# Mixer B's softmax division on GpSimd instead of VectorE

## The chip, the cores and the metric

The kernel runs on one core of one Trainium2 chip. The metric is the device time of one execution in microseconds (us), given as the median of several runs. Engines are named as in the profile: PE is TensorE (its matmuls; PEld its weight loads), DVE is VectorE, ACT is ScalarE, POOL is GpSimd, SP is SyncE, whose queue issues most of the DMAs.

## The reference

A two-layer encoder on 512 tokens of width 1024. Layer 0 mixes tokens by dilated window attention (mixer A), layer 1 by multi-head latent attention (mixer B). Each mixer is followed by a dense squared-ReLU MLP. The change is in mixer B alone, and of it only in the last three lines:

```python
def mla_mixer(h, w_in, q_a_gain, w_qb, kv_a_gain, w_kvb, q_gain, k_gain, w_o):
    lat = h @ w_in                                   # c_q (256), c_kv (128), k_rope (64)
    ...
    q = (rms_norm(c_q, q_a_gain) @ w_qb).reshape(B, S, 8, 192)
    kv = (rms_norm(c_kv, kv_a_gain) @ w_kvb).reshape(B, S, 8, 256)
    ...                                              # per-head RMS norm of q and k, rotary part of 64
    def attend(qblk):
        s = jnp.einsum('bqhd,bkhd->bhqk', qblk, k).astype(jnp.float32) * scale
        p = jax.nn.softmax(s, axis=-1)
        return jnp.einsum('bhqk,bkhd->bqhd', p.astype(v.dtype), v)
```

The output of the 8 heads goes through `w_o`, is added to the input, and the second MLP follows.

## The kernel before

Everything is float32. Products that need full precision are split into a high and a low part (`whi`, `wlo` and the like), three matmuls each. Tiles of 128 rows; the 512 tokens are four row blocks `r`.

**Mixer B.** The 8 heads are worked as four pairs `p` of two heads `h`. For each pair there are, per row block, a projection of keys and values (`kv_chunk`, three matmuls of 512 columns) and one of queries (`q_chunk`, six matmuls of 384 columns), both at line 1032 into the two PSUM banks `sc`. ACT takes the squares for the norm (L1043 for queries, L137 for keys), DVE adds a constant (L129, `rs_v`), POOL raises to the power -1/2 (L132: `rqs` for queries, `krs` for keys). DVE and POOL then make the rotary parts (queries: L1050, L1053 on DVE, `rd` at L1057 on POOL; keys: `ks` at L1086 on DVE, `kd` at L1088 on POOL). PE transposes them (L124 into the two banks `tp`), and ACT and DVE write them as high and low parts (`qn`, `qr`, `kn`, `kr`, L1069 to L1103).

**One step of attention** is one head and one row block, 32 steps in all. `score` does five matmuls (L1114) into a bank `acc`; DVE reduces the maximum (L1116) and scales it (L1117); ACT takes the exponential into the SBUF tile `pe` and its sum (L1119); DVE inverts the sum (L1120) and multiplies `pe` by it (L1121). Three steps later `part2` has PE transpose `pe` (four matmuls of 128x128 at L124 into a bank `acc`), and DVE (even `r`) or ACT (odd `r`) copies the result to `pTs` (L1132, L1130). After the fourth row block of a head, `pv_b` multiplies by the values (L1138) and ACT and DVE write the two parts of `oB` (L1140, L1141; named `hT` in the profile). `pe` has three buffers. The four banks `acc` are shared by scores, transposes and values; in the last pair the scores use `sc` and the rest `tp`, because `acc` then holds the output projection `w_o` (L185), which runs between the steps as far as its weights are split (L157 ACT, L158 DVE).

**Order.** The code gives an order of calls (the table `plan` puts the next pair's projections between the steps of this one), but each engine's final order is chosen by a scheduler when the program is built; it may move an instruction ahead of others on its engine, and it decides anew when an operation changes its engine. On the chip each engine then works strictly in that order and waits where an input or a buffer is not ready. In the names below a number marks one use of a buffer: `pe_8842` is one step's tile, `acc_8985` one use of a bank.

Of the kernel before, what the change touches and what calls it, by code (L numbers as in the profile page):

```python
# [13 lines left out]
ALU = mybir.AluOpType  # L14
# [73 lines left out]
def encoder_kernel(ctx: ExitStack, tc: tile.TileContext, x, norm_mix, norm_ffn, a_w_qkv, a_q_gain, a_k_gain,  # L88
# [3 lines left out]
    V, A, G, PE = nc.vector, nc.scalar, nc.gpsimd, nc.tensor  # L92
# [3 lines left out]
    def nm(s):  # L96
        uid[0] += 1
        return f"{s}_{uid[0]}"
# [24 lines left out]
    def transpose(o, i):  # L123
        PE.transpose(o, i, ident)  # L124
# [826 lines left out]
    if True:  # L951
        with tc.tile_pool(name="bpool", bufs=1, reuse_waits="tile") as bp, \
# [66 lines left out]
            def bank(d, which):  # L1019

                pool, tag = {"s": (sc_p, "sc"), "p": (tp_p, "tp"), "o": (tp_p, "tp")}[which] \
                    if d["p"] == HB // 2 - 1 else (acc_p, "acc")
                return pool.tile([P, 512], F32, tag=tag, name=nm(tag))
# [82 lines left out]
            def score(d, h, r):  # L1106

                qn, qr, kn, kr = d["qn"][r], d["qr"][r], d["kn"], d["kr"]
                rq = d["rq"][:, r, h:h + 1]
                sc = bank(d, "s")  # L1110
                ops = [(qn[:, h, 0], kn[:, h, 0]), (qn[:, h, 0], kn[:, h, 1]), (qn[:, h, 1], kn[:, h, 0]),
                       (qr[:, h], kr[:, h, 0]), (qr[:, h], kr[:, h, 1])]
                for i, (lt, rt) in enumerate(ops):
                    PE.matmul(sc, lhsT=lt, rhs=rt, start=(i == 0), stop=(i == 4))  # L1114
                mx = st.tile([P, 4], F32, tag="bmx", name=nm("bmx"))
                V.tensor_reduce(mx[:, 0:1], sc, axis=AX.X, op=ALU.max)  # L1116
                V.tensor_scalar(mx[:, 1:2], mx[:, 0:1], rq, -1.0, op0=ALU.mult, op1=ALU.mult)  # L1117
                pe = bw.tile([P, S], F32, tag="pe", name=nm("pe"), bufs=3)
                A.activation(pe, sc, AF.Exp, bias=mx[:, 1:2], scale=rq, accum_out=mx[:, 2:3])  # L1119
                V.reciprocal(mx[:, 3:4], mx[:, 2:3])  # L1120
                V.tensor_scalar(pe, pe, mx[:, 3:4], None, op0=ALU.mult)  # L1121

                def part2(pT):
                    tp = bank(d, "p")
                    for j in range(NT):
                        transpose(tp[:, j * P:(j + 1) * P], pe[:, j * P:(j + 1) * P])
                    tv = tp.rearrange("p (j t) -> p j t", j=NT)
                    dst = pT[:, :, r * P:(r + 1) * P]
                    if r % 2:
                        A.activation(dst, tv, AF.Copy)  # L1130
                    else:
                        V.tensor_copy(dst, tv)  # L1132
                return part2
# [27 lines left out]
            for s_ in range(HB * NT + lag):  # L1161
                p, c = divmod(s_, 8)
                if s_ < HB * NT:
                    if c == 0 and p:
                        cur = nxt
                    pend.append((cur, c // 4, c % 4, score(cur, c // 4, c % 4)))
                if s_ >= lag:
                    d, h2, r2, f = pend.pop(0)
                    if r2 == 0:
                        if pTs is None:  # L1170
                            pTs = x16.tile([P, 2, NT, S], F32, tag="x16", name="pTs")
                        pT = pTs[:, h2]
                    f(pT)
                    if r2 == NT - 1:
                        pv_b(d, h2, pT)
                if p + 1 < HB // 2:
                    if c == 2:
                        nxt = new_pair(p + 1)
                    if s_ < NT - 1:
                        tail = tail + [q_chunk(cur, s_ + 1)]  # L1180
                    fresh = [fn(nxt, r) for fn, r in plan.get(c, [])]
                    if c == 7:
                        tail, fresh = tail + fresh, []
                    for f in tail:
                        f()
                    tail = fresh
# [40 lines left out]
```

## Time and profile before

| | us |
|---|---|
| median of 3 runs (lowest, highest) | 1428.91 (1428.28, 1428.96) |
| span of the profiled execution | 1425.8 |
| what lies between the two | 3.1 |
| PE busy | 1394.0 (98%) |
| DVE, ACT, POOL busy | 939.6, 740.5, 217.2 |
| mixer B's attention, about | 925 to 1060 of the span |

No time is listed for the profiled execution but its span; the 3.1 us beside it are the median less that span. The granted TensorE clock was full in every slice. A matmul's end is modelled and overlaps the next one's start, so idle time of PE shorter than about 0.15 us does not show. The useful measure of PE is the spacing in the chain of work, where five score matmuls take 1.16 us although each is listed with 390 ns.

### The profile page before, as it was taken

The page shows a single profiled execution, that of the slowest core. Times are in us where ns is not written, and L with a number is a line of the kernel's source. Part 1 is how long each engine was busy: PE and PEld are TensorE (multiplying, and loading weights), DVE is VectorE, ACT ScalarE, POOL GpSimd, SP SyncE. Part 2 cuts the span into 40 slices and gives each one's busy share as a digit, 9 for nine tenths or more (in the row PEclk, how much of TensorE's full clock was granted, in tenths as well). Part 3 has the DMA queues.
Part 4 walks back from the last instruction along what each step waited for, and adds up shares of the span by engine and source line. Part 5 has one row for each costly group of instructions (what it writes and reads, how often), then busy time and mean ns, then how long its engine had stood idle before and what let it go on. Part 6 is the DMA issues. An engine that isn't in the chain of part 4 may idle for free.

```text
span 1425.8 us, 19234 instructions
## 1 busy us (share of the span) xinstructions
PE 1394.0 (98%) x7044; PEld 1183.8 (83%) x7044; DVE 939.6 (66%) x1497; ACT 740.5 (52%) x1594; POOL 217.2 (15%) x240
## 2 busy tenths in 40 slices
PE   7999999999999999999999999999999999999998
PEld 7999888988888988888888887777768888888886
DVE  6886768676886754465564759788745365575647
ACT  6554656464564623553545446677633553544543
POOL 1110212021112001020010203433201020020201
PEclk9999999999999999999999999999999999999999
DMA  9535222322322335668493844200115658394835
GB/s 323 166 134 168 75 87 87 107 89 75 118 61 77 121 134 195 174 133 222 116 233 99 206 120 91 82 31 30 44 40 163 183 127 231 93 234 128 192 90 118
DMA packets 121086, 185.25 MB, mean 130 GB/s; under 512 B 8416, under 2 KB 58336, under 8 KB 120992
## 3 DMA queue, kind: packets, MB, share of 16 engines
q1 hardware_dynamic: 101808, 144.96, 31.6%
q0 software_dynamic: 19184, 39.07, 15.2%
q8 instruction: 55, 0.90, 0.3%
q14 instruction: 39, 0.32, 0.1%
HBM read 176.13 MB, written 7.86 MB: 129 GB/s over the span
## 4 chain that ended last, share of the span: by engine, by line
PE 89%; DVE 6%; ACT 2%; issue 1%; DMA 1%; POOL 0%; SPq 0%; DVEq 0%; ACTq 0%; POOLq 0%
PE acc L185 51%; PE sc L852 11%; PE tp L852 7%; PE tp L124 4%; PE sc L421 3%; PE acc L1138 1%; PE sc L1032 1%; PE acc L1114 1%; PE tp L421 1%; DVE wlo L796 1%; PE sco L701 1%; PE sc L587 1%; PE acc L421 1%; PE sco L697 1%; DVE wlo L407 1%
## 5 line engine op out<-in xcount | busy, mean ns | idle before, releaser
L185 PE MATMUL acc<-whi,hT 128*128 128x512 f32 (+2 forms) x1216 | 384.2, 390 | 2.2 <-ACT hT L739 1.3
L185 PE MATMUL acc<-hT_f,whi 128*128 128x512 f32 (+1 forms) x1152 | 318.7, 366 | 1.7 <-DVE resid L915 1.2
L158 DVE TENSOR_TENSOR wlo<-raw,whi 128x1024 fp32r<-128x1024 f32 (+3 forms) x146 | 172.4, 1189 | 180.2 <-ACT whi L157 179.9
L185 PEld LDWEIGHTS acc<-whi,hT 128*128 128x128 f32 x1216 | 225.4, 188 | 42.0 <-ACT hT L739 1.9
L185 PEld LDWEIGHTS acc<-hT_f,whi 128*128 128x128 f32 x1152 | 208.1, 189 | 37.4 <-DVE resid L915 1.6
L185 PE MATMUL acc<-wlo,hT 128*128 128x512 f32 (+2 forms) x608 | 235.9, 388 | 0.0
L157 ACT ACTIVATE whi<-raw 128x1024 fp32r<-128x1024 f32 (+3 forms) x146 | 149.7, 1031 | 161.5 <-PE acc L185 64.1
L796 DVE TENSOR_TENSOR wlo<-wqs,whi 128x1024 fp32r<-128x1024 f32 x112 | 137.9, 1232 | 113.4 <-ACT whi L795 113.4
L185 PE MATMUL acc<-hT_f,wlo 128*128 128x512 f32 (+1 forms) x576 | 204.9, 366 | 0.0
L795 ACT ACTIVATE whi<-wqs 128x1024 fp32r<-128x1024 f32 x112 | 118.8, 1061 | 161.3 <-PE acc L185 65.8
L852 PE MATMUL sc<-whi,asp 128*128 128x512 f32 x512 | 164.9, 390 | 0.8 <-DVE resid L826 0.7
L781 POOL DMA_DIRECT2D wqs<-in_ffn_w_dram x64 | 77.6, 1344 | 546.1 <-DVE wlo L796 362.4
L185 PEld LDWEIGHTS acc<-wlo,hT 128*128 128x128 f32 x608 | 114.4, 188 | 18.7 <-issue 0.2
L185 PEld LDWEIGHTS acc<-hT_f,wlo 128*128 128x128 f32 x576 | 108.5, 189 | 17.4
L852 PE MATMUL tp<-whi,asp 128*128 128x512 f32 x352 | 112.2, 390 | 1.8 <-DVE resid L826 1.8
L852 PEld LDWEIGHTS sc<-whi,asp 128*128 128x128 f32 x512 | 96.1, 188 | 21.4 <-issue 1.5
L132 POOL TENSOR_TENSOR qrs<-rs_v,nhalf 128x4 f32<-128x4 f32 x48 | 58.7, 1228 | 288.8 <-DVE rs_v L129 239.7
L852 PE MATMUL sc<-wlo,asp 128*128 128x512 f32 x256 | 99.6, 389 | 0.0
L137 ACT ACTIVATE junk<-acc 128x128 f32<-128x128 f32 x192 | 53.0, 276 | 56.4 <-PE acc L185 51.4
L852 PEld LDWEIGHTS tp<-whi,asp 128*128 128x128 f32 x352 | 66.1, 188 | 16.4 <-DVE resid L826 2.7
L852 PE MATMUL tp<-wlo,asp 128*128 128x512 f32 x176 | 68.2, 389 | 0.0
L295 ACT ACTIVATE qkT<-tp 128x512 f32<-128x512 f32 x48 | 35.8, 765 | 51.2 <-PE tp L124 50.9
(231 smaller groups left out, 2185.3 us busy)
## 6 DMA issues: line engine op xcount, KB each, us to landing
wqs<-in_ffn_w_dram SPq DMA_DIRECT2D x80, 512.0 KB, 5.1
raw<-in_ffn_w_dram SPq DMA_DIRECT2D x64, 512.0 KB, 4.5
wqs<-in_ffn_w_dram POOLq DMA_DIRECT2D x64, 512.0 KB, 7.5
raw<-in_a_w_qkv_dram SPq DMA_DIRECT2D x96, 256.0 KB, 3.1
b<-in_a_w_qkv_dram SPq DMA_DIRECT2D x24, 384.0 KB, 5.7
vall<-vo POOLq DMA_DIRECT2D x24, 192.0 KB, 2.2
raw<-in_a_w_o_dram SPq DMA_DIRECT2D x8, 512.0 KB, 3.8
raw<-in_b_w_o_dram SPq DMA_DIRECT2D x8, 512.0 KB, 3.7
```

The costliest lines, as they stand in the source:

```text
L124: PE.transpose(o, i, ident)
L132: G.tensor_tensor(out, v[:, :n], nhalf[:, :n], op=ALU.pow)
L137: A.activation(junk, x, AF.Square, scale=1.0 / math.sqrt(dim), accum_out=out)
L157: A.activation(hi[:, :nk, :n], raw[:, :nk, :n], AF.Copy)
L158: V.tensor_tensor(lo[:, :nk, :n], raw[:, :nk, :n], hi[:, :nk, :n].bitcast(F32), op=ALU.subtract)
L185: PE.matmul(accs[o][:, oc], lhsT=lt, rhs=rt, start=(kt == 0 and p_i == 0 and hv == 0), stop=(kt == total - 1 and p_i == 2), skip_group_che ...
L295: A.activation(dst, tv, AF.Copy)
L421: PE.matmul(banks[t][:, :VH], lhsT=lt, rhs=rt[:, j], start=(first and k == 0 and i_ == 0), stop=(k == 3 and i_ == 2), skip_group_check=True)
L781: marks["sum"] = nc.gpsimd.dma_start(t, src, accum_op=ALU.add).ins
L795: A.activation(hi, x, AF.Copy)
L796: V.tensor_tensor(lo, x, hi.bitcast(F32), op=ALU.subtract)
L852: PE.matmul(bk[t], lhsT=lt, rhs=rt[:, j], start=(first and k == 0 and i_ == 0), stop=(k == 3 and i_ == 2), skip_group_check=True)
```

## The change

The multiplication by the inverse sum, on DVE before, is issued on POOL. It reads and writes the SBUF tile `pe`; the operations of DVE that read PSUM stay where they are.

```diff
                 A.activation(pe, sc, AF.Exp, bias=mx[:, 1:2], scale=rq, accum_out=mx[:, 2:3])
                 V.reciprocal(mx[:, 3:4], mx[:, 2:3])
-                V.tensor_scalar(pe, pe, mx[:, 3:4], None, op0=ALU.mult)
+                G.tensor_scalar(pe, pe, mx[:, 3:4], None, op0=ALU.mult)
```

POOL gets 32 instructions and DVE loses 32; ACT keeps its 984 rows and SP's queue is the same, row by row. The scheduler's order differs through mixer B's attention and for a few rows where the second MLP begins. Three places matter below.

First place: DVE during the first steps of pair 0. `bmx` holds a step's maximum and sum, `qn` and `rs_v` belong to the query and key projections.

```order
 L1120 RECIPROCAL bmx_8182<-bmx_8182 128x1
-L1121 TENSOR_SCALAR pe_8185<-pe_8185,bmx_8182 128x512
 L1116 TENSOR_REDUCE bmx_8229<-acc_8223 128x1
 L129 TENSOR_SCALAR rs_v_8377<-kss_8374,ssr 128x2
+L1117 TENSOR_SCALAR bmx_8229<-bmx_8229,rqs_75 128x1
 L1116 TENSOR_REDUCE bmx_8276<-acc_8270 128x1
 L1070 SCALAR_TENSOR_TENSOR qn_8343<-tp_8338,gn,qn_8343 128x2x128
 L129 TENSOR_SCALAR rs_v_8394<-kss_8391,ssr 128x2
-L1117 TENSOR_SCALAR bmx_8229<-bmx_8229,rqs_75 128x1
```

The multiplication is gone from the head of the queue, and the scaling of the second step's maximum stands four rows earlier.

Second place: the end of pair 1's first head. On PE, `acc_8985` holds the transposes of that head's last row block, `acc_8991` its product with the values (PV), `acc_9032` a score, `sc_8869` the first query projection of pair 2.

```order
 L1114 MATMUL acc_8972<-kr_8284,qr_8659 128x512 x2
 L124 MATMUL acc_8985<-ck,pe_8780 128x128 x4
+L1138 MATMUL acc_8991<-pTs,vb_8285 128x512 x4
+L1114 MATMUL acc_9032<-kn_8283,qn_8669 128x512 x3
+L1114 MATMUL acc_9032<-kr_8284,qr_8670 128x512 x2
+L124 MATMUL acc_9045<-ck,pe_8842 128x128 x4
 L1032 MATMUL sc_8869<-whi_8750,cT 128x384
 L1032 MATMUL sc_8869<-wlo_8751,cT 128x384
```

The PV, the score and the transposes behind it moved ahead of the projection. On ACT at the same place (`hT_8026` is the output of that PV, `junkb_8876` and `qs_8883` read the projection):

```order
 L1130 ACTIVATE pTs<-acc_8985 128x4x128
 L1102 ACTIVATE kr_8740<-tp_8892 128x2x128
-L1043 ACTIVATE junkb_8876,qss_8877<-sc_8869 128x192 x2
-L1047 ACTIVATE qs_8883<-sc_8869 128x256
 L1119 ACTIVATE pe_8981,bmx_8978<-acc_8972,bmx_8978,rqs_76 128x512
 L1140 ACTIVATE hT_8026<-acc_8991 128x512
+L1043 ACTIVATE junkb_8876,qss_8877<-sc_8869 128x192
+L1119 ACTIVATE pe_9041,bmx_9038<-acc_9032,bmx_9038,rqs_76 128x512
+L1043 ACTIVATE junkb_8876,qss_8877<-sc_8869 128x192
+L1047 ACTIVATE qs_8883<-sc_8869 128x256
```

The three readings of the projection moved behind the PV's output, and an exponential stands between them. The same exchange happens one pair later (`sc_9290`, the first query projection of pair 3).

Third place: PE towards the end of pair 3's first head, whose PV is `tp_9657`; `tp_9651` are the transposes of its last row block, `pe_9590`.

```order
+L124 MATMUL tp_9632<-ck,pe_9564 128x128 x4
+L1114 MATMUL sc_9619<-kn_9160,qn_9447 128x512 x3
+L1114 MATMUL sc_9619<-kr_9161,qr_9448 128x512 x2
 L1114 MATMUL sc_9638<-kn_9160,qn_9500 128x512 x3
 L1114 MATMUL sc_9638<-kr_9161,qr_9501 128x512 x2
+L124 MATMUL tp_9651<-ck,pe_9590 128x128 x4
 L1138 MATMUL tp_9657<-pTs,vb_9162 128x512 x4
```

Before, `tp_9651` stood ten matmuls of `w_o` and a score ahead of that PV; now it stands right in front of it. A little earlier the last query projection, `sc_9472`, moved from in front of pair 2's last PV to behind it.

## The prediction

> **What bounds the kernel now.** I read the page's span first, then the busy times by stage (columns: stretch, busy us and count of PE, PEld, DVE, ACT, POOL, then the clock), because only mixer B's attention is touched.
>
> ```profile
> span 1425.8 us, 19234 instructions
> ```
>
> ```profile
> 925.00:935.00 10.00, 8.85 (x46) 6.69 (x44) 9.22 (x28) 7.18 (x26) 3.80 (x6) 1.00 0.01 2
> 935.00:960.00 25.00, 25.00 (x130) 19.06 (x128) 22.12 (x69) 19.50 (x67) 9.73 (x14) 1.00 0.13 43
> 960.00:975.00 15.00, 13.80 (x67) 10.02 (x65) 13.76 (x38) 11.02 (x35) 4.08 (x6) 1.00 0.10 35
> 975.00:985.00 10.00, 9.28 (x56) 7.86 (x56) 7.68 (x22) 7.53 (x26) 2.85 (x4) 1.00 0.01 2
> 985.00:1005.00 20.00, 18.79 (x95) 14.12 (x95) 18.23 (x51) 14.90 (x48) 5.51 (x8) 1.00 0.11 32
> 1005.00:1020.00 15.00, 15.00 (x73) 10.67 (x72) 11.36 (x35) 10.35 (x34) 6.31 (x9) 1.00 0.09 32
> 1020.00:1062.00 42.00, 40.63 (x185) 30.56 (x183) 22.86 (x51) 15.97 (x32) 0.74 (x1) 1.00 0.15 50
> sum 137.00, PE 131.34 PEld 98.98 DVE 105.24 ACT 86.45 POOL 33.02; mean PE 18.76 PEld 14.14 DVE 15.03 ACT 12.35 POOL 4.72
> ```
>
> PE is busy 131.3 of 137 us, so it is the bound, and DVE is next: over nine tenths busy in three stretches. POOL has room. What PE waits for in 925 to 1060 (us in total, times, longest):
>
> ```profile
> PE sc L1032 <- DVE ks L1086: 2.4, 2, 1.2
> PE acc L1114 <- ACT pe L1119: 1.1, 1, 1.1
> PE tp L1138 <- ACT pTs L1130: 0.7, 1, 0.7
> PE sc L1032 <- DVE r L1053: 0.5, 1, 0.5
> PE tp L124 <- DVE kr L1103: 0.2, 1, 0.2
> ```
>
> This is all that a lighter DVE can give back: 2.4 + 0.5 + 0.2 us behind DVE itself, and 1.1 us behind an exponential that waited for DVE's L1117. At most 4.2 us, 0.3% of the kernel, although DVE loses far more.
>
> **What moves: 32 multiplications.** On DVE they took (ns, least/median/most):
>
> ```profile
> L1121 DVE TENSOR_SCALAR pe<-pe,bmx x32: 468/486/1044, 928.3 to 1054.1; 128x512 f32<-128x512 f32 x32
> ```
>
> At the median that is 32 x 0.486 = 15.6 us off DVE, nearly all of it beside PE's work. On POOL the trace has no such operation. The nearest rows:
>
> ```profile
> L993 POOL TENSOR_TENSOR krr<-krr,kr x4: 322/326/328, 903.5 to 912.8; 128x64 f32<-128x64 f32 x4
> L1088 POOL TENSOR_TENSOR kd<-krr,krs x12: 613/614/616, 924.8 to 1006.0; 128x256 f32<-128x256 f32 x12
> L1057 POOL TENSOR_TENSOR rd<-rt,r x13: 729/735/740, 925.6 to 1021.5; 128x256 f32<-128x256 f32 x13
> L132 POOL TENSOR_TENSOR rqs<-rs_v,nhalf x12: 696/705/867, 938.3 to 1018.7; 128x2 f32<-128x2 f32 x12
> L972 POOL TENSOR_SCALAR sgB<-sgB x1: 873/873/873, 874.2 to 874.2; 128x256 f32<-128x256 f32 x1
> ```
>
> From 64 to 256 elements POOL takes 614 - 326 = 288 ns more, 1.5 ns an element; 512 elements come to 614 + 256 x 1.5 = 1.0 us. The one TENSOR_SCALAR gives twice 873 ns, 1.75 us, at the high end; the low end is DVE's own 0.49. I take 1.0, since L1088 lies in this stage and has twelve samples, and L972 works on runs of 32 elements with gaps. 32 x 1.0 us raise POOL from 33 to 65 of 137 us: not a bound on average. A step's multiplication ends 0.5 us later, and its transposes come two to three steps later, so that latency is covered but for the very last step:
>
> ```profile
> 1054.13 0.49 DVE L1121 TENSOR_SCALAR pe<-pe,bmx 128x512 f32<-128x512 f32 x1
> ...
> 1055.37 0.60 PE L124 MATMUL tp<-ck,pe 128*128 128x128 f32 x4
> 1056.01 0.60 ACT L1130 ACTIVATE pTs<-tp 128x512 f32<-128x512 f32 x1 [1.21 <-PE tp L124]
> 1056.66 3.70 PE L1138 MATMUL tp<-pTs,vb 128*128 128x512 f32 x8 [0.69 <-ACT pTs L1130]
> ```
>
> Done at 1054.62, wanted at 1055.37: 0.75 us of cover, made of four matmuls of `w_o`. With 1.0 us it costs 0, with 1.75 about 0.5. In front of `krs`, `rqs`, `kd` and `rd` in POOL's queue a multiplication now stands; who waits behind it is `ks` on DVE and the transposes of `kd` and `rd`.
>
> **The port.** Two rows of the trace show POOL holding DVE up:
>
> ```profile
> L129 DVE TENSOR_SCALAR rs_v<-kss,ssr x11: 205/220/600, 929.4 to 1004.8; 128x2 f32<-128x2 f32 x11
> ...
> 930.47 0.61 POOL L1088 TENSOR_TENSOR kd<-krr,krs 128x256 f32<-128x256 f32 x1
> 930.51 0.60 DVE L129 TENSOR_SCALAR rs_v<-kss,ssr 128x2 f32<-128x2 f32 x1
> ```
>
> An `rs_v` that normally takes 0.22 us began while `kd` ran and ended with it, after 0.60. L1121's own maximum of 1044 against 486 is the same effect, and goes. In exchange 32 us of POOL work lie over 23 `rs_v` and nine `wlo` splits: at a quarter of the time (32 of 137) and half an operation each, 32 x 0.23 x 0.5 = 3.7 us of DVE, from the 15.6 freed. I put it at 0 on PE, with +2 as the high end should half of it hit a wait. [...]
>
> **What the new order costs.** Each engine's order changed with the engine, and this is where I see the sum. Spacings and places come from the chain and the timeline:
>
> ```profile
> 968.89 0.60 PE L124 MATMUL acc<-ck,pe 128*128 128x128 f32 x4
> ...
> 970.35 0.61 ACT L1130 ACTIVATE pTs<-acc 128x512 f32<-128x512 f32 x1
> ...
> 970.69 0.41 PE L1032 MATMUL sc<-whi,cT 128*128 128x384 f32 x1 [1.20 <-DVE ks L1086]
> ...
> 971.83 3.60 PE L1138 MATMUL acc<-pTs,vb 128*128 128x512 f32 x8
> ...
> 972.09 0.33 ACT L1043 ACTIVATE junkb<-sc 128x192 f32<-128x192 f32 x1 [0.73 <-PE sc L1032]
> ...
> 975.46 0.60 ACT L1140 ACTIVATE hT<-acc 128x512 fp32r<-128x512 f32 x1 [1.46 <-PE acc L1138]
> ```
>
> ```profile
> 980.20 0.30 PE L124 MATMUL tp<-ck,qs 128*128 128x128 f32 x1 [0.20 <-DVE kr L1103]
> ```
>
> ```profile
> 981.34 1.28 PE sc L1032 x6
> ...
> 990.37 3.43 PE acc L1138 x8
> 993.81 1.17 PE acc L1114 x5
> ...
> 1010.43 1.05 PE sc L1032 x6
> ...
> 1055.53 0.45 PE tp L124 x4
> ```
>
> *First steps of pair 0: -0.3.* The scaling of the maximum now stands ahead of a reduction and no multiplication delays it, so the exponential frees its bank in time and the 1.1 us wait goes. About 0.8 us come back some steps later, where DVE's new order puts `ks` behind a reduction and behind an inverse that waits for an exponential: followed row by row with the spacings above, PE wants that `ks`'s bank at 937.3 and DVE frees it at 938.1. Ends: -1.1 and +1.1.
>
> *End of pair 1's first head: +1.3.* Today PE stands until 970.69 for a bank, projects (1.05 us), and the PV follows at 971.83. In the new order the PV comes at once, but it needs the copy that ACT ends at 970.35 + 0.61, so it starts at 971.0: the wait stays, with ACT in place of DVE. Projection `sc_8869` follows after 3.43 + 1.17 + 0.45 (four transposes) at 976.05 and ends at 977.1. ACT, which squared it during the PV from 972.09, now stands through the PV and begins at 977.2, with an exponential between the squares. The next projections wait for its buffers: the two waits at 980.2 and 981.34 (0.2 and 0.5 us) become roughly 0.6, 0.7 and 0.5 us, and I get the projection of 981.34 at 982.7. Ends: -0.5 (the waits vanish on the lighter DVE) and +2.5.
>
> *End of pair 2 and pair 3: +1.4.* The same exchange shifts pair 2's last PV about 0.4 us earlier, but a whole projection of 1.05 us now comes after it. Pair 3's transposes of the fourth row block stand directly before the PV; the last PV of the profile shows what that costs, 1.21 us of ACT waiting and 0.7 of PE (1055.98 to 1056.66). Sum -0.4 + 1.05 + 0.7. Ends: 0 and +2.5.
>
> *The rest.* SP's queue is unchanged, POOL issues no DMA before the multiplications end, and the few moved rows of the second MLP lie among matmuls without waits: 0, give or take 0.5.
>
> Sum: -0.3 + 1.3 + 1.4 = +2.4 us. On the profiled execution 1425.8 becomes 1428.2; the runs' median lies 3.1 above that span, so 1428.91 + 2.4 = 1431.3.
>
> **The rivals.**
> *Faster.* The lighter DVE decides: all four waits on DVE go and the order costs nothing, 1428.9 - 4.2 = 1424.7. For it: DVE's 9.22 of 10 and 13.76 of 15 us. Against: at 970 the copy on ACT ends when it did, whatever DVE does. It decides where ACT's work before that copy had been waiting for DVE.
> *No change.* The new order loses in one place what it wins in another, as at pair 0: 1428.9, give or take 1.4. For it: PE's work is the same, 131.3 of 137 us, and the moves are small. That the multiplications do not leave DVE is excluded by the order.
> *Slower, POOL becomes the wait.* At 1.75 us `rd` in the queue behind two multiplications comes 0.75 us later than at 1.0, against PE's want of it at about the time it is ready, in each of three pairs, the last step loses 0.5, collisions 2: 2.4 + 2.25 + 0.5 + 2 = +7.15, 1436.1. It decides from about 1.3 us per multiplication on, where 0.75 us of cover ends. Against: POOL idles half the stage even so.
>
> **How the numbers follow.** Forecast 0.48, no change 0.27, POOL wait 0.16, faster 0.09. A measurement of this kernel tells about 0.2%, 2.9 us, from no change, so below 1426.05 is faster and above 1431.77 slower. The forecast's own range, 1429.5 to 1433.5, lies across that edge; four tenths of it, 0.19, are above. Slower: 0.19 + 0.16 = 0.35. Same: 0.29 + 0.27 = 0.56. Faster: 0.09. The range leaves out the faster rival's far half and half of the POOL wait: 1426.5 to 1435.5.
>
> **What would show it.** Right: L1121 on POOL near 1.0 us; DVE's busy time in the stage down by some 12 to 15 us; PE's wait for `ks` gone and one for ACT's `pTs` (L1130) in front of the PVs in its place; more PE idle time between 975 and 985. Wrong: multiplications of 1.3 us and more, PE waiting for POOL's `rd` or `kd`, `rs_v` often at 0.6 us or above; or PE's idle time down to 2 us, which is the faster rival.

## Result: 4.4 us slower, by the order of the work

The changed kernel takes 1433.31 us (median of 5 runs, 1432.68 to 1434.35) against 1428.91 before: +4.4 us, a ratio of 1.0031 with the interval 1.002 to 1.0042. The forecast was 1431.3, in the same direction with about half the size. The profiled execution has a span of 1431.2 us, 1432.97 in all. Three runs of the experiments below lasted 2007 to 8034 us, for a reason that is not on record; the intervals leave them out, and they shift three of the medians by under 0.15 us.

The stage, in the same windows as before and 4 us more, since it ends at 1066 here (stretch, then busy us and count of PE, PEld, DVE, ACT, POOL; clock; DMA share and rate):

```profile
925.00:935.00 10.00, 9.68 (x52) 7.75 (x51) 8.86 (x27) 7.85 (x30) 7.79 (x9) 1.00 0.01 2
935.00:960.00 25.00, 24.04 (x123) 17.96 (x121) 19.25 (x63) 19.66 (x64) 20.86 (x22) 1.00 0.15 43
960.00:975.00 15.00, 13.49 (x63) 9.55 (x62) 10.00 (x26) 9.66 (x29) 11.14 (x9) 1.00 0.13 35
975.00:985.00 10.00, 8.61 (x52) 7.28 (x51) 6.69 (x23) 6.84 (x27) 6.16 (x9) 1.00 0.01 2
985.00:1005.00 20.00, 18.86 (x96) 13.89 (x94) 16.00 (x41) 15.47 (x51) 13.83 (x13) 1.00 0.10 27
1005.00:1020.00 15.00, 13.97 (x66) 10.01 (x67) 9.95 (x33) 8.65 (x30) 10.80 (x12) 1.00 0.12 36
1020.00:1062.00 42.00, 40.31 (x187) 30.93 (x186) 19.88 (x44) 17.30 (x37) 13.93 (x10) 1.00 0.16 51
1062.00:1066.00 4.00, 3.31 (x10) 1.58 (x9) 0.69 (x1) 0.60 (x1) 0.00 (x0) 1.00 0.00 0
sum 141.00, PE 132.27 PEld 98.94 DVE 91.30 ACT 86.03 POOL 84.51; mean PE 16.53 PEld 12.37 DVE 11.41 ACT 10.75 POOL 10.56
```

DVE went from 105.2 us to 91.3: 13.9 us lighter, as forecast. POOL went from 33.0 to 84.5 us. Yet PE has more idle time, 8.7 us in all against 5.7: in the stretch 1005 to 1020, for one, it was busy for all 15 us, and now for 13.97. What PE waits for, from 925 to 1066 (us in total, times, longest):

```profile
PE acc L1138 <- ACT pTs L1130: 3.1, 2, 1.5
PE tp L1138 <- ACT pTs L1130: 1.4, 2, 0.7
PE tp L124 <- DVE kr L1103: 1.1, 2, 0.6
...
PE sc L1032 <- ACT junkb L1043: 0.6, 1, 0.6
PE acc L1114 <- DVE qr L1073: 0.6, 1, 0.6
...
PE tp L124 <- POOL pe L1121: 0.3, 1, 0.3
```

The 2.4 us for `ks` and 1.1 us for the exponential are gone. In their place stand 4.5 us of waits for ScalarE's copy of the transposed probabilities (L1130), directly ahead of four PVs (L1138), where only the last PV waited before (0.7 us), and small waits behind DVE. Of the whole list only the last row shown here names GpSimd. The moved operation itself (ns, least/median/most):

```profile
L1121 POOL TENSOR_SCALAR pe<-pe,bmx x32: 1562/1568/2071, 928.3 to 1057.7; 128x512 f32<-128x512 f32 x32
```

It takes 1.57 us where VectorE took 0.49. The places that the forecast spoke of, from the timeline (start, us, engine, line, operation; in brackets the wait and its releaser):

```profile
970.08 0.65 ACT L1130 ACTIVATE pTs<-acc 128x512 f32<-128x512 f32 x1
...
970.78 3.70 PE L1138 MATMUL acc<-pTs,vb 128*128 128x512 f32 x8 [1.51 <-ACT pTs L1130]
...
975.84 0.42 PE L1032 MATMUL sc<-whi,cT 128*128 128x384 f32 x1
...
977.24 0.33 ACT L1043 ACTIVATE junkb<-sc 128x192 f32<-128x192 f32 x1 [2.13 <-PE sc L1032]
...
979.73 0.41 PE L1032 MATMUL sc<-whi,cT 128*128 128x384 f32 x1 [0.65 <-ACT junkb L1043]
...
981.50 0.64 PE L124 MATMUL tp<-ck,qs 128*128 128x128 f32 x2 [0.49 <-DVE kr L1103]
...
982.70 0.45 PE L1032 MATMUL sc<-whi,cT 128*128 128x384 f32 x1 [0.23 <-DVE r L1053]
...
1057.71 1.56 POOL L1121 TENSOR_SCALAR pe<-pe,bmx 128x512 f32<-128x512 f32 x1 [3.45 <-DVE bmx L1120]
...
1059.33 0.66 PE L124 MATMUL tp<-ck,pe 128*128 128x128 f32 x4 [0.32 <-POOL pe L1121]
...
1060.67 1.55 PE L1138 MATMUL tp<-pTs,vb 128*128 128x512 f32 x3 [0.69 <-ACT pTs L1130]
```

The reader sees a trade at 970: the PV now starts 1.05 us earlier than before, but behind a wait of its own. The projection that used to come first starts at 975.84, ScalarE stands 2.13 us until it has something to square, and the lateness travels down the queries' chain to 982.70.

### The profile page after: what moved, and what is told of

Its sections match the earlier page's. It is cut to its first block, busy times and chain, and to the rows that moved or that the text cites. A ratio compares the mean times of both kernels' runs of the same rounds, so it can differ in the third digit from the quotient of the medians.

```text
span 1431.2 us, 19271 instructions
## 1 busy us (share of the span) xinstructions
PE 1395.6 (98%) x7044; PEld 1184.4 (83%) x7044; DVE 925.3 (65%) x1465; ACT 739.5 (52%) x1594; POOL 268.5 (19%) x272
## 4 chain that ended last, share of the span: by engine, by line
PE 88%; DVE 6%; ACT 3%; issue 1%; DMA 1%; POOL 0%; SPq 0%; ACTq 0%; DVEq 0%
PE acc L185 52%; PE sc L852 11%; PE tp L852 7%; PE tp L124 4%; PE sc L421 3%; PE acc L1138 1%; PE acc L1114 1%; PE tp L421 1%; DVE wlo L796 1%; PE sc L1032 1%; PE sco L701 1%; PE sc L587 1%; PE acc L421 1%; PE sco L697 1%; ACT pe L1119 1%
## 5 line engine op out<-in xcount | busy, mean ns | idle before, releaser
L158 DVE TENSOR_TENSOR wlo<-raw,whi 128x1024 fp32r<-128x1024 f32 (+3 forms) x146 | 172.2, 1187 | 179.4 <-ACT whi L157 165.1
L157 ACT ACTIVATE whi<-raw 128x1024 fp32r<-128x1024 f32 (+3 forms) x146 | 149.7, 1030 | 160.0 <-PE acc L185 71.9
```

The source lines that it names most:

```text
L157: A.activation(hi[:, :nk, :n], raw[:, :nk, :n], AF.Copy)
L158: V.tensor_tensor(lo[:, :nk, :n], raw[:, :nk, :n], hi[:, :nk, :n].bitcast(F32), op=ALU.subtract)
```

## Experiments

The question is which of three things costs the 4.4 us: the **order** in which every engine now gets its work (the scheduler chose another one when the operation changed engine), **GpSimd** (1.57 us per multiplication, its queue, its collisions with VectorE), less whatever a **lighter VectorE** gives back. Engine and order can be set apart. Each instruction has the same number in both kernels, so an order can be pinned from outside, with edges that fix the issue order and add no wait:

```diff
+    for names in want.values():        # one list each for PE, VectorE, ScalarE, GpSimd
+        for a, b in zip(names, names[1:]):
+            tc.add_manual_dep(by[f"I-{b}"], f"I-{a}", ... NoSync ...)   # b is issued behind a
```

The 32 multiplications are in no list, so the scheduler places them among the fixed rest. The pins themselves add next to nothing: the pinned kernels with the division on VectorE list 19232 to 19237 instructions, the kernel before 19234.

### Engine and order apart: a table of six

On GpSimd, in the order of before:

```diff
-                V.tensor_scalar(pe, pe, mx[:, 3:4], None, op0=ALU.mult)
+                G.tensor_scalar(pe, pe, mx[:, 3:4], None, op0=ALU.mult)
+    want = lists of the kernel before
```

> The multiplications run on GpSimd as in the change, but PE, VectorE and ScalarE get every instruction in exactly the order of the kernel before (order edges without waits; the multiplications themselves are left free in GpSimd's queue). If the cost of the change is the new order (my reading), nearly all of it goes: 1426 to 1429.5 us, and the PV of pair 1's first head again starts some 1.1 us after the copy it needs. If the cost is GpSimd's 1.57 us per multiplication, by latency or by collisions with VectorE, the time stays at 1432 to 1433.5, with PE waiting for transposes of pe or for rd and kd. If the relief of VectorE were worth what stood behind it, 1424.7.

On VectorE, in the order of the changed kernel (the kernel before, with `want` = lists of the changed kernel):

> The multiplications run on VectorE as before, but PE, VectorE and ScalarE get every other instruction in exactly the order of the changed kernel. If the order costs the 4.4 us: 1432 to 1434 (a little over the change, if the relief of VectorE helps at all), with ScalarE's copy L1130 in front of the PVs. If GpSimd's duration or its collisions cost them: 1428.5 to 1430.

The line L1121 left out, in the one order and in the other:

> The multiplication is left out (the probabilities stay undivided, so the output differs); the rest is in exactly the order of the kernel before. It bounds what a lighter VectorE can bring without GpSimd's load. If the waits behind VectorE (4.2 us) are all VectorE's throughput: 1424.7. By my reading only a part of them: 1426 to 1428.5. What GpSimd's own work costs is the difference to GpSimd in the same order: near 0 by the order theory, 3 us or more by the GpSimd theory.

> The multiplication is left out (the probabilities stay undivided, so the output differs); the rest is in exactly the order of the changed kernel. By the order theory it is about as slow as the change, 1431.5 to 1433.5, though GpSimd has nothing to do and VectorE is lighter. By the GpSimd theory 1428 or less.

Medians in us; the four new kernels had 5 to 11 runs each and shared 25 runs of the kernel before (1428.89). In parentheses the interval of the ratio to it:

| division | order of before | order of the changed kernel |
|---|---|---|
| on VectorE | 1428.9 (the kernel before) | 1434.6 (1.0024 to 1.0051) |
| on GpSimd | 1430.1 (1.0 to 1.0018) | 1433.3 (the change; 1.002 to 1.0042) |
| left out | 1427.9 (0.9982 to 1.0) | 1432.8 (1.0014 to 1.0034) |

Across a row the order costs 5.7, 3.2 and 4.9 us. Down a column the engine matters by 2.2 us at most. The new order is slow with no GpSimd work at all, and in that order GpSimd's multiplications cost 0.5 us over none, less than the intervals resolve. Two kernels came out 0.6 us above the ranges expected of them: on GpSimd in the old order 1430.1 and not 1426 to 1429.5, for which the queue below accounts, and on VectorE in the new order 1434.6 and not 1432 to 1434. With the division on VectorE and the new order, PE's list of waits, 925 to 1066, begins as that of the changed kernel does:

```profile
PE acc L1138 <- ACT pTs L1130: 3.1, 2, 1.5
PE tp L124 <- DVE kr L1103: 1.6, 3, 0.7
PE tp L1138 <- ACT pTs L1130: 1.4, 2, 0.7
PE acc L1114 <- DVE qr L1073: 0.9, 1, 0.9
```

So the order is shown to be the cause. Read along the row of the change, 3.2 of its 4.4 us go when the old order is put back; the other 1.2 (interval 0 to 2.6) are left to GpSimd in the old order. The table holds two more readings.

**A lighter VectorE is worth about 1 us (interval 0 to 2.6), not 4.2.** Without the multiplications, in the old order, PE's waits are these:

```profile
PE sc L1032 <- ACT vb L1084: 2.1, 2, 1.0
PE acc L1114 <- ACT pe L1119: 0.9, 1, 0.9
```

The wait for `ks` went from 2.4 to 2.1 us and changed its name. The bank that PE stood for is freed by two readers, and in the kernel before they end 0.07 us apart, at 970.47 and 970.54:

```profile
970.09 0.38 ACT L1084 ACTIVATE vb<-sc 128x256 f32<-128x256 f32 x1
970.13 0.41 DVE L1086 TENSOR_TENSOR ks<-sc,krs 128x256 f32<-128x256 f32 x1
```

The list of waits names the last one only.

**On GpSimd in the old order a real queue forms.** The wait for `ks` grows from 2.4 to 3.5 us. Its cause in that kernel's timeline:

```profile
965.24 3.11 POOL L1121 TENSOR_SCALAR pe<-pe,bmx 128x512 f32<-128x512 f32 x2 [2.56 <-DVE bmx L1120]
...
968.25 1.22 DVE L158 TENSOR_TENSOR wlo<-raw,whi 128x1024 fp32r<-128x1024 f32 x1
968.31 1.75 POOL L132 TENSOR_TENSOR krs<-rs_v,nhalf 128x2 f32<-128x2 f32 x1
...
970.09 0.42 DVE L1086 TENSOR_TENSOR ks<-sc,krs 128x256 f32<-128x256 f32 x1 [0.62 <-POOL krs L132]
```

The inverse `krs` stands behind two multiplications, 3.11 us, and then beside `wlo`, where it takes 1.75 us in place of 0.70.

### The queue on GpSimd

Two edges: at both places `krs` is issued ahead of the second of the two multiplications.

```diff
+    want also holds [krs of pair 1, 2nd multiplication ahead of it], [krs of pair 2, the same]
```

> Multiplications on GpSimd with the order of the kernel before on PE, VectorE and ScalarE (1430.1 us when only that is done), and at two places in GpSimd's queue the inverse krs (L132) now stands ahead of the second of two multiplications instead of behind both. If the 1.2 us over the kernel before are krs waiting behind 3.1 us of multiplications, and VectorE's ks and PE behind it, PE's wait for ks falls from 3.5 to about 2.3 and the time to 1428.7 to 1429.3. If they are collisions of GpSimd with VectorE at the memory, or the last multiplication's latency alone (0.5), it stays at 1429.6 to 1430.4.

Measured: 1428.37 us against 1429.02 before (ratio 0.9999, 0.999 to 1.0008), and 1.7 us below the kernel without the two edges. The two come from different sets of runs, and their intervals against the kernel before overlap, so the times alone don't prove the gain; the lists of waits show it, where PE's two waits for `sc` go from 3.5 to 2.0 us in all. The time is 0.3 us below the range expected of it. At the place shown above:

```profile
966.46 0.72 POOL L132 TENSOR_TENSOR krs<-rs_v,nhalf 128x2 f32<-128x2 f32 x1
967.17 1.58 POOL L1121 TENSOR_SCALAR pe<-pe,bmx 128x512 f32<-128x512 f32 x1
967.80 1.22 DVE L158 TENSOR_TENSOR wlo<-raw,whi 128x1024 fp32r<-128x1024 f32 x1
...
969.50 0.41 PE L1032 MATMUL sc<-whi,cT 128*128 128x384 f32 x1 [1.03 <-ACT vb L1084]
```

PE's wait is 1.03 us again and behind ScalarE. The move took `krs` out from behind the multiplication and out from beside `wlo` at once, so how the gain divides between queue and collision stays open.

### Where in the order the time goes

The differences fall into pieces that can be exchanged one at a time. On VectorE, with the lists of before but for one part:

> The multiplications stay on VectorE; the order is that of the kernel before, but for pair 0's steps (both heads' 8 row blocks, up to the PV at 957), which have the changed kernel's order on all engines. My prediction put this part at -0.3 (with the relief of VectorE). By the trace of the whole new order on VectorE the PV of 957.23 comes 0.8 later and that of 971.83 at the same time, so: 1428.5 to 1429.7. If the cost is spread over all the order's moves evenly, 1430.8.

> As before, but for the end of pair 1's first head (the PV of 971.83 ahead of the query projection that stood before it, and the eleven small moves after it up to 990), which have the changed kernel's order. My prediction put this place at +1.3; the trace of the whole new order on VectorE shows +2.6 between the PVs of 971.8 and 990.2. So 1430.2 to 1431.5. By the theory that only the last pair costs, 1428.9.

> As before, but for pair 2's end and pair 3 (from the transposes ahead of the PV of 1015.63 to the last PV), which have the changed kernel's order. My prediction put it at +1.4; the trace of the whole new order shows +2.0. So 1430.3 to 1431.5. If what is lost here is only shifted from an earlier place (the engines arriving late), it would cost nothing by itself: 1428.9.

> As before, but for the end of pair 2's first head (the PV of 1004.81 ahead of the query projection that stood before it), which has the changed kernel's order: the third place of the exchange, for which my prediction had no term. By the trace of the whole new order on VectorE it costs about 0.1 (2.6 late at 990.2 and 2.7 at 1015.6): 1428.7 to 1429.4. If the four parts add up to the whole order's 5.3 us, with 0.9, 1.3 and 2.1 measured for the other three, it is 1.0: 1430.

> As before, but with the changed kernel's order in both of the last two parts together: the end of pair 2's first head, and pair 2's end with pair 3. Alone they measured 2.3 and 2.1 us. If the losses are separate, 4.4 us: 1433.5. If the moves at pair 2's end take over the late query chain that the first exchange leaves (in the trace of the whole new order the two places together lose 2.1 us), 1431 to 1431.8.

| part in the new order | median, us | before | difference | ratio, interval |
|---|---|---|---|---|
| A: pair 0 | 1429.89 | 1429.02 | +0.9 | 0.9996 to 1.0013 |
| B: end of pair 1's first head | 1430.29 | 1429.02 | +1.3 | 0.9999 to 1.0016 |
| C: end of pair 2's first head | 1431.45 | 1429.16 | +2.3 | 1.001 to 1.0028 |
| D: end of pair 2, pair 3 | 1431.15 | 1429.02 | +2.1 | 1.0007 to 1.0024 |
| C and D together | 1431.33 | 1428.97 | +2.4 | 1.0005 to 1.0024 |

A and B alone are inconclusive by their intervals, though their traces show the waits; A lies 0.2 us above the range expected of it, B and D inside theirs. Part C missed my expectation (0.1 us, or 1.0 if the parts add up) by more than 1 us: I had read its price off a trace in which D follows. C and D together cost what either costs alone; a sum of 4.4 us lies outside the interval. By the lists of waits the moves of D take over the lateness that C leaves: with C alone PE waits 0.7 us behind `junkb` and 1.4 behind `kr`, with both not at all and 0.7. The timeline of C alone shows how one exchange of a PV and a projection costs more than its wait:

```profile
1003.68 3.70 PE L1138 MATMUL acc<-pTs,vb 128*128 128x512 f32 x8 [1.55 <-ACT pTs L1130]
...
1010.14 0.33 ACT L1043 ACTIVATE junkb<-sc 128x192 f32<-128x192 f32 x1 [2.12 <-PE sc L1032]
...
1012.72 0.41 PE L1032 MATMUL sc<-whi,cT 128*128 128x384 f32 x1 [0.73 <-ACT junkb L1043]
...
1016.56 0.30 PE L124 MATMUL tp<-ck,qs 128*128 128x128 f32 x1 [1.23 <-DVE kr L1103]
```

PE waits 1.55 us ahead of the PV, which it did for the projection before. ScalarE then idles 2.12 us through the PV, and the squares that come late hold PE up for another 0.73 and 1.23 us. A, B, and C with D sum to 4.6 us of the whole order's 5.7; with intervals of 2 to 4 us each, the missing 1.1 is not a finding.

### What the remaining wait is worth

If ScalarE's `vb` and VectorE's `ks` hold that bank together, the cure is in their queues. Ahead of both stands one rounding of the weights of the output projection, `whi` (L157) and `wlo` (L158), which nobody needs yet:

```diff
 ScalarE   ... vb (third) | - whi | kn | kr | junkb | pe | junkb | vb (fourth) ... pe | + whi | hT
 VectorE   ... bmx | - wlo | ks | kn ... inverse | multiplication | + wlo | hT
```

Both are moved to where the two engines idle during the PV, in pairs 1 and 2; the rest has the order of before. Once with the division on VectorE, once on GpSimd with `krs` first:

> Multiplications on VectorE and the order of the kernel before, but at the two places where PE waits 1.2 us for ks (and, 0.1 us earlier, for ScalarE's vb), one rounding of w_o (whi L157, 1.09 us on ScalarE) stands after the exponential L1119 of the PV's time instead of ahead of vb, and its remainder (wlo L158, 1.3 us on VectorE) after the inverse and multiplication there instead of ahead of ks. If that wait is the order of ScalarE's and VectorE's queues, and not VectorE's load, the 2.4 us go: 1426.4 to 1427. If the wait moves to the copy L1130 or to the new place of whi and wlo: 1428 to 1429.

> The same move in the kernel with the multiplications on GpSimd, the order of the kernel before and krs ahead of the second multiplication. The remaining 2.0 us of waiting for vb go: 1426 to 1427, beside the kernel with the multiplications on VectorE and this move. If a lighter VectorE is worth more once the queue's order is mended, it is faster than that one by 0.5 to 1 us; if it is not, the two are the same within 0.4.

Measured: 1427.30 us on VectorE (ratio 0.9987, 0.9978 to 0.9996) and 1426.62 on GpSimd (0.9984, 0.9975 to 0.9993), against 1429.16. The first lies 0.3 us above the range expected for it (1426.4 to 1427), the second inside. The waits behind `ks` and `vb` are gone from both lists of waits. With the division on GpSimd the list, from 925 to 1066, begins like this, and what follows is 0.3 and below:

```profile
PE acc L1114 <- ACT pe L1119: 0.7, 1, 0.7
PE acc L185 <- ACT hT L1140: 0.7, 1, 0.7
PE tp L1138 <- ACT pTs L1130: 0.7, 1, 0.7
PE acc L1138 <- ACT pTs L1130: 0.6, 2, 0.3
PE sc L1032 <- DVE r L1053: 0.5, 1, 0.5
```

The second kernel beats the kernel before by 2.5 us and the change by 6.7 (the latter from two sets of runs). It owes that to the order: the same move on VectorE brings 1.9, and the 0.7 us between the two are within their intervals.

## Why the forecast was right, and where not

*What bounds, and what relief is worth.* Right in kind: PE is the bound, DVE lost 13.9 us and PE gained next to nothing. The "at most 4.2 us" was far too high a bound: leaving the multiplications out altogether brought 1.0.

*The price on GpSimd.* This step failed: 1.0 us, extended from two-input rows of 64 and 256 elements, against 1.57 measured. The upper end, 1.75 from the one row of the same operation, was nearer. It is the one sign of a wrong forecast (1.3 us and more) that came true; the others stayed away.

*Tail.* Put at 0 with a price of 1.0, at 0.5 with 1.75. PE stood 0.5 us ahead of the last head's last transposes at 1059.33, for the L1121 that ended at 1059.27: the four matmuls of `w_o` before them start 1.49 us earlier, and 1.01 in the kernel before (the 0.32 in brackets counts from their modelled end). The failed price is most of this miss: 1.57 - 0.49, less the 0.75 us of cover, makes 0.33.

*First steps of pair 0: -0.3.* The PV of 957.23 starts at 957.01, so -0.2. That is luck as far as the traces tell: six executions with the old order up to there and the division on VectorE start this PV anywhere from 956.95 to 958.14. The 1.1 us wait did go, but what came back was not `ks`: PE waits for `qr` (0.6), for `bmx` (0.4) and for `qn` (0.3). On VectorE itself part A measured +0.9, within its interval of no change.

*End of pair 1's first head: +1.3.* Right in size and in its steps: PV forecast at 971.0 and found at 970.78, projection at 976.05 and 975.84, ScalarE's square at 977.2 and 977.24, waits of 0.6, 0.7 and 0.5 found as 0.65, 0.49 and 0.23, the next projection at 982.7 and found at 982.70. By the next PV (990.21 before, 991.63 now) the kernel is 1.4 late, 1.6 more than at the PV of 957; alone on VectorE the part measured +1.3.

*End of pair 2 and pair 3: +1.4.* Mis-sized. From the PV of 990 to the last one the kernel loses another 2.6 us (1.42 to 4.01), of which 0.5 is the tail: 2.1, as D measures by itself. The terms 1.05 + 0.7 held: from pair 2's last PV to pair 3's first it is 32.90 us (1017.18 to 1050.08) where it was 31.08 (1015.63 to 1046.71), +1.8. The -0.4 ahead of them did not come: pair 2's last PV is 1.55 late after 1.42, +0.1, with 0.63 us of waiting for `kr` just before it. The exchange at the end of pair 2's first head, for which the sum had no term, costs 2.3 alone; that it does not come on top of D was luck for the sum.

*Collisions (headed "The port" in the prediction): 0 on PE.* In the new order GpSimd's whole load costs 0.5 us, no more than the tail, so 0 fits there, as far as the intervals resolve it; the keys' `rs_v` stayed at 0.22 us in the median and 0.43 at most. The direction was not right: I looked for VectorE's `rs_v` held by GpSimd, and the costly case is GpSimd's `krs` beside VectorE's `wlo`. In the kernel with GpSimd in the old order `wlo` ran from 968.25 to 969.47, and `krs`, 0.70 us in the median of before, began at 968.31 and ended at 970.06, 0.59 us behind it. In the changed kernel two `krs` begin 0.04 and 0.05 us behind a `wlo`, at 968.63 and 1003.25; they took 1.76 and 1.74 us, where the median of the stage's eleven is 0.72. What the two engines share there, a port or something else, no run shows.

*The rivals.* "The lighter DVE decides" and "no change" are out. "POOL becomes the wait" named `rd` behind two multiplications and a threshold of 1.3 us. The threshold was passed, but no wait of PE for `rd` or `kd` came. A queue of that kind did form, with the inverse `krs` in it, and costs 1.2 us in the old order. In the changed kernel it is there too and hidden:

```profile
965.56 3.10 POOL L1121 TENSOR_SCALAR pe<-pe,bmx 128x512 f32<-128x512 f32 x2 [3.56 <-DVE bmx L1120]
968.63 1.76 POOL L132 TENSOR_TENSOR krs<-rs_v,nhalf 128x2 f32<-128x2 f32 x1
```

There the PV comes ahead of the projection that needs the bank, and that projection starts at 975.84 without a wait.

*The sum.* +2.4 forecast, +4.4 measured. By the last PV the trace has 4.0 of it: -0.2, +1.6, +2.1 and the tail's +0.5, where -0.3, +1.3, +1.4 and 0 were forecast. The measurement's interval (2.9 to 6.0) holds both 4.0 and 4.4.

## What to carry to other kernels

When an operation changes its engine under a scheduler, the order of everything near it changes too: compare the orders first, and measure engine and order apart by pinning the one while changing the other. A wait is worth only the distance to its second-latest releaser (here 0.07 us of a wait of 1.2), so look up who else frees the same buffer before counting the wait as a gain. Small operations that others wait for belong ahead of long ones in a slow engine's queue (here `krs`: PE's waits for `sc` went from 3.5 to 2.0 us), and work that nobody waits for belongs where its engine idles (here `whi` and `wlo`: 1.9 us with the division on VectorE).

## What was not expected of the hardware

GpSimd's one-input multiplication of 128x512 took 1.57 us, 3.2 times VectorE's 0.49, and stayed between 1.56 and 1.58 in the kernel with `krs` first.

TensorE's granted clock fell to 0.50 for 3.4 us at the start of the second MLP (1094.7 to 1098.2), in the changed kernel's profile and not in that of before. Here are two stretches after the same wait, of after and then of before (busy us and matmuls, PE first; the clock is the number behind POOL):

```profile
1095.00:1096.00 1.00, 0.92 (x5) 0.92 (x6) 0.69 (x3) 0.00 (x0) 0.23 (x1) 0.50 1.05 406
1097.00:1098.00 1.00, 1.00 (x7) 1.00 (x6) 1.00 (x2) 0.00 (x0) 0.00 (x0) 0.50 1.00 363
```

```profile
1091.00:1092.00 1.00, 0.92 (x8) 0.92 (x9) 0.69 (x3) 0.23 (x1) 0.24 (x1) 1.00 1.05 406
1093.00:1094.00 1.00, 1.00 (x11) 1.00 (x10) 1.00 (x2) 0.00 (x0) 0.00 (x0) 1.00 1.07 373
```

It belongs to the execution, not to the change: eight of the fourteen traces have the fall here and six have not, among them kernels on either engine, and from the last PV to the end the eight take 370.4 to 370.7 us and the six 369.1 to 369.2. One of the changed kernel's five runs had a mean clock of 1.000 too. Of the 100 runs of the kernel before that stood beside the experiments, 16 had a mean clock of 1.000 and averaged 1428.1 us, 83 had 0.998 or 0.999 and averaged 1429.2, and one had 0.949 and took 1430.65. In the trace of part C, on VectorE, the fall lasts 3.4 us too (1094.2 to 1097.6); what makes the clock fall was not shown. The drop also bears on the spans: 1431.2 - 1425.8 = 5.4 us between the two profiled executions are the 4.0 us of the attention and 1.4 of the clock. So the profiled span of before, at a clock of 1.000, lay 3.1 us under the median, where that of after lies 2.1 under its own; some 1.8 us of either lie outside the span in most runs. Spans of single executions are good to about 1 us, and differences of that size need the runs.
